# Eight SBUF places laid 448 bytes further, at another offset within a 512-byte line

## The chip, the cores and the metric

The kernel runs on one core of one Trainium2 chip. The metric is the device time of one execution in microseconds (us). TensorE (PE) does the matrix products; VectorE (DVE), ScalarE (ACT) and GpSimd (POOL) prepare operands and take results away; SyncE (SP) issues most DMAs. SBUF, the working memory, has 128 partitions; an array has the same byte address in each of them.

## The reference

One layer on 512 frames of width 1024, in float32:

```python
u = rms_norm(h, g_mix); z = u @ w_in            # q, k, v of two attentions, forget logits, two gates
y_a = sliding_window_attention(...) @ w_br_swa
y_b = forgetting_attention(...) @ w_br_fox
mixed = gates[0] * y_a + gates[1] * y_b
h = h + mixed @ w_mix_out                       # the merge's output projection
u = rms_norm(h, g_mlp)
h = h + jnp.square(jax.nn.relu(u @ w_ff1)) @ w_ff2
h = h + sigmoid(rms_norm(h, g_ple) @ w_ple_gate) * (p @ w_ple_proj)
return rms_norm(h, g_final)
```

## The kernel before

Every float32 product is done as three products of rounded parts: an operand is split into a high part (a rounded copy, made by ACT) and a low part (the rest, made by DVE), and PE computes high x high, high x low and low x high into the same PSUM tile (`mm3`, lines 72 to 75). A matmul has a stationary operand of 128 columns, which PE loads ahead of it, and a moving operand of up to 512 columns, which it streams. In the trace's names (out <- moving, stationary) the moving operand stands first.

The order of PE's and POOL's instructions is the order of the code; the other engines are scheduled by the framework, but for stretches in which their order is also the code's. The stages in order of time, with the names that PE's rows have:

- normalisation and the v projections, to 46 us (`va`, `vb`);
- both attentions (`h_sc`, `h_tr`, `h_pv`), filled up with the other projections (`pf`), to 214 us;
- branch projections (`psy`, moving `attn`) and half of the gates (`g`), to 298 us. The gates go through seven products instead of eight per 2x2 of blocks; the operands of products 3 and 7 (`u1_3`, `u1_7`) lie in four of the eight places named below, those of 5 and 6 elsewhere;
- the merge's output projection (`psm`), from 298 to 346 us: `mix` stationary, split weights of `w_mix_out` moving;
- embedding projection (`pspp`), to 359 us; its results lie in four of the eight places and go to HBM (`pp_spill`);
- the MLP, to 679 us: four rounds of ff1 (`f1`, split weights stationary, normed input moving, 256 columns) and ff2 (`s_..x`, `s_..y`, `s_..z`: the squared results `o2` of ff1 stationary, split weights of `w_ff2` moving, 512 columns); both in seven products. A step of ff1 has 24 matmuls, a step of ff2 has 12, and there are 56 steps of each;
- the embedding's gate (`psgt`, `psgl`), final norm and output.

The places that the change touches are eight buffers of 4096 bytes per partition in a pool of their own, each found by a tag `d0` to `d7`:

```python
    at2 = ctx.enter_context(tc.tile_pool(name="at2", bufs=1))
...
                mix[i] = at2.tile([P, 2, S], F32R, tag=f"d{i}", name=f"mix_{i}")
...
    OP_PLACE = {(0, 1): 0, (0, 5): 0, (0, 7): 0, (1, 1): 1, (1, 5): 1, (1, 7): 1, (0, 4): 2,
                (1, 4): 3, (0, 2): 4, (1, 2): 5, (1, 3): 5, (1, 6): 6, (0, 3): 7, (0, 6): None}
...
            t = at2.tile([P, 2, 2, 256], F32R, tag=f"d{n}", name=f"o2_{g}_{pn}")
```

`mix` and all of ff1's results lie there, but for the operand of product 6 in every other group of ff2 (`None` above: it lies in a buffer of another pool). The multiplication in ff2 is

```python
            for j in range(2):
                for n, (o, w) in enumerate(((oh, wh), (oh, wl), (ol, wh))):
                    nc.tensor.matmul(ps, o[:, j, ts_], w[:, j, :],
```

so `o` is stationary and `w` moving. The pools are laid one behind the other in SBUF, and within a pool a tag gets its place when it is first used. This gives every array an offset within a 512-byte line of its partition (its byte address modulo 512). Since slices are stepped by 512 bytes or multiples, an array keeps this offset in all its matmuls.

Of the kernel before, what the change touches and what calls it, by code (L numbers as in the profile page):

```python
# [8 lines left out]
F32 = mybir.dt.float32  # L9
# [5 lines left out]
P = 128  # L15
# [34 lines left out]
def layer_kernel(ctx: ExitStack, tc: tile.TileContext, x, p, g_mix, w_in, b_forget, swa_sinks,  # L50
# [794 lines left out]


    at2 = ctx.enter_context(tc.tile_pool(name="at2", bufs=1))
    look["wp2"] = ctx.enter_context(tc.tile_pool(name="wp2", bufs=2))
    look["split"] = 2
    n_mm = [0]  # L850
# [137 lines left out]
    for t in P2_STEPS:  # L988
# [8 lines left out]
        i = unit_of[t]  # L997
# [310 lines left out]
    for n, st_ in enumerate(steps):  # L1308
        res = None
        if done is not None:  # L1310
            if done[0] == "f1":
                res = win_out(done[:2], done[2], tmp)
                if res is not None:
                    src, dst, i, e = res
# [137 lines left out]
```

## Time and profile before

| what | value |
|---|---|
| median of three runs | 735.4 us (732.38, 735.40, 737.94) |
| the profiled execution, its own time | 736.25 us |
| its span in the trace | 734.2 us |
| outside the span | 2.05 us |
| granted clock, mean over the span | 0.998 of full speed |

The trace shows one execution, the one of 736.25 us. A matmul's row has a start and a duration; matmuls overlap, so the time that one costs is the distance from its start to the start of the next (called its spacing here), not its duration.

### The profile page before, as it was taken

Reading aid. Unit: us, or ns where it says so; the run is one execution under the profiler, and the core shown is the slowest. Engines: PE = TensorE matmul, PEld = TensorE weight load, DVE = VectorE, ACT = ScalarE, POOL = GpSimd, SP = SyncE. Lnnn points to the kernel's source line nnn. Section 1 sums busy time; section 2 is a strip of 40 time slices with the busy share of each in tenths; the row PEclk is TensorE's granted clock in tenths of the full one; section 3 lists DMA queues with packets and bytes.
Section 4 is the critical chain, followed back from the end, with each engine's and each line's share of the span. In section 5 each row is a group of like instructions: output and inputs, shape, how many; then the busy total and the mean of one; then the engine's idle time right before and its main releaser. Section 6 shows DMA issues by size and latency. Waiting matters only on the chain.

```text
span 734.2 us, 11456 instructions
## 1 busy us (share of the span) xinstructions
PE 721.4 (98%) x4234; PEld 635.9 (87%) x4234; DVE 530.7 (72%) x898; ACT 449.5 (61%) x838; POOL 86.2 (12%) x127
## 2 busy tenths in 40 slices
PE   9999999999999999999999999999999999999995
PEld 7998888888888998888889889988999889988884
DVE  4576888777697556546769985898669966997564
ACT  5457788879853553334777635774477546875452
POOL 1010211100001200002410102010300021010101
PEclk9999999999999999999999999999999999999999
DMA  8346455670364894530795598738894689069002
GB/s 254 93 131 160 113 145 145 151 194 1 116 217 99 172 344 145 200 115 19 234 211 197 107 276 171 224 88 248 185 252 111 153 225 226 33 144 341 4 25 90
DMA packets 73465, 116.72 MB, mean 159 GB/s; under 512 B 6593, under 2 KB 43969, under 8 KB 73410
## 3 DMA queue, kind: packets, MB, share of 16 engines
q1 hardware_dynamic: 65346, 86.64, 37.4%
q0 software_dynamic: 8064, 29.36, 21.0%
q8 instruction: 33, 0.54, 0.3%
q14 instruction: 22, 0.18, 0.1%
HBM read 72.93 MB, written 4.19 MB: 105 GB/s over the span
## 4 chain that ended last, share of the span: by engine, by line
PE 94%; DVE 2%; ACT 2%; DMA 1%; issue 1%; POOL 0%; POOLq 0%; DVEq 0%; ACTq 0%
PE pf L73 5%; PE pf L75 5%; PE pf L74 5%; PE s_6x L1269 3%; PE s_4x L1269 3%; PE s_2x L1269 3%; PE s_0x L1269 3%; PE h_sc L729 2%; PE h_pv L799 2%; PE h_tr L787 2%; PE psy L73 2%; PE psy L75 2%; PE psy L74 2%; PE psm L74 2%; PE psm L75 2%; PE psm L73 2%
## 5 line engine op out<-in xcount | busy, mean ns | idle before, releaser
L297 POOL DMA_DIRECT2D wq<-wq x26 | 23.5, 941 | 177.5 <-DVE u154l L324 27.1
L747 ACT ACTIVATE s<-s,h_nm 128x128 f32<-128x128 f32 (+1 forms) x64 | 32.6, 511 | 5.9 <-DVE h_nm L740 5.2
L358 POOL TENSOR_SCALAR n_ms<-acc 128x1 f32<-128x1 f32 x15 | 5.7, 381 | 171.3 <-ACT junk L1049 101.8
L70 DVE TENSOR_TENSOR h_ptl<-h_tr,h_pth 128x512 fp32r<-128x512 f32 (+2 forms) x40 | 22.9, 604 | 4.0 <-ACT h_pth L69 3.4
L69 ACT CAST u_h<-n_tr 128x512 fp32r<-128x512 f32 x22 | 12.2, 584 | 15.5 <-PE n_tr L378 7.6
L70 DVE TENSOR_TENSOR u_l<-n_tr,u_h 128x512 fp32r<-128x512 f32 x22 | 14.6, 686 | 8.2 <-ACT u_h L69 8.2
L69 ACT CAST h_pth<-h_tr 128x512 fp32r<-128x512 f32 (+2 forms) x40 | 19.4, 523 | 1.8 <-PE h_tr L787 1.4
L787 PE MATMUL h_tr<-ident,s 128*128 128x128 f32 x136 | 19.6, 277 | 0.2
L1049 ACT ACTIVATE junk<-h_sb 128x512 f32<-128x512 f32 x16 | 10.1, 629 | 15.6 <-DVE h_sb L1039 13.1
L297 POOL DMA_DIRECT2D wgw<-wgw x8 | 7.1, 970 | 101.7 <-DVE u25l L324 77.7
L1039 DVE TENSOR_TENSOR h_sb<-psm,h_sb 128x512 f32<-128x512 f32 x8 | 5.5, 690 | 16.4 <-PE psm L75 16.4
L799 PE MATMUL h_pv<-h_pth,v 128*128 128x256 f32 (+1 forms) x64 | 17.3, 291 | 0.0
L799 PE MATMUL h_pv<-h_ptl,v 128*128 128x256 f32 (+1 forms) x64 | 16.9, 305 | 0.4 <-DVE h_ptl L70 0.3
L787 PEld LDWEIGHTS h_tr<-ident,s 128*128 128x128 f32 x136 | 15.0, 141 | 2.0 <-DVE h_ao L809 0.5
L1358 DVE TENSOR_TENSOR sgp<-sgp,pp 128x512 f32<-128x512 f32 (+1 forms) x9 | 5.7, 633 | 15.2 <-ACT sgp L1357 15.2
L767 ACT ACTIVATE s<-s,h_rec 128x128 f32<-128x128 f32 (+2 forms) x32 | 14.2, 483 | 2.3 <-DVE h_rec L761 2.3
L809 DVE TENSOR_TENSOR h_ao<-h_pv,h_ao 64x512 f32<-64x512 f32 x16 | 10.9, 681 | 6.0 <-ACT h_ao L808 5.8
L735 DVE CUSTOM_DVE_ANT_0 s<-h_sc,causal 128x128 f32<-128x128 f32 (+3 forms) x32 | 13.8, 483 | 0.3 <-PE h_sc L729 0.3
L799 PEld LDWEIGHTS h_pv<-h_ptl,v 128*128 128x128 f32 x64 | 12.1, 188 | 1.7 <-DVE h_ptl L70 0.8
L1357 ACT ACTIVATE sgp<-psgt,rs 128x512 f32<-128x512 f32 x7 | 4.8, 685 | 14.2 <-PE psgt L75 14.2
L761 DVE RECIPROCAL h_rec<-h_den 128x4 f32<-128x4 f32 x16 | 3.0, 185 | 14.5 <-ACT s L747 14.3
L799 PEld LDWEIGHTS h_pv<-h_pth,v 128*128 128x128 f32 x64 | 12.1, 189 | 0.9
(1744 smaller groups left out, 2952.4 us busy)
## 6 DMA issues: line engine op xcount, KB each, us to landing
wq<-in_w_ff_dram SPq DMA_DIRECT2D x45, 512.0 KB, 5.5
wq<-wq POOLq DMA_DIRECT2D x26, 512.0 KB, 5.4
wq_c<-in_w_ff_dram SPq DMA_DIRECT2D x9, 512.0 KB, 6.2
wg<-in_w_in_dram SPq DMA_DIRECT2D x4, 1024.0 KB, 5.5
wgw<-in_w_in_dram SPq DMA_DIRECT2D x8, 512.0 KB, 4.9
wgw<-wgw POOLq DMA_DIRECT2D x8, 512.0 KB, 5.7
wmix<-in_w_mix_out_dram SPq DMA_DIRECT2D x4, 1024.0 KB, 5.3
wpg<-in_w_ple_gate_dram SPq DMA_DIRECT2D x4, 1024.0 KB, 9.4
```

The costliest lines, as they stand in the source:

```text
L69: nc.scalar.copy(hi, src)
L70: nc.vector.tensor_tensor(lo, src, hi.bitcast(F32), ALU.subtract)
L73: nc.tensor.matmul(ps, lh, rh, start=start, stop=False)
L74: nc.tensor.matmul(ps, lh, rl, start=False, stop=False)
L75: nc.tensor.matmul(ps, ll, rh, start=False, stop=stop)
L297: nc.gpsimd.dma_start(q, other, accum_op=ALU.add)
L729: nc.tensor.matmul(ps[:, off:off + n], qs[i][z][:, qb * P:(qb + 1) * P], kk[i][z][:, k0:k0 + n], start=z == 0, stop=z == 1)
L747: nc.scalar.activation(sl, sl, AF.Exp, bias=nm[:, qb:qb + 1], accum_out=den[:, qb:qb + 1])
L767: nc.scalar.activation(sl, sl, AF.Copy, scale=rec[:, qb:qb + 1])
L787: nc.tensor.transpose(tr[:, n, :], c["s"][:, o, :], ident)
L799: nc.tensor.matmul(pv[:, q0:q0 + nq, :], V2[kb][:, c["v"], :], t[:, o:o + nq, :], start=n == 0, stop=n == 2 * NT - 1, skip_group_check=True)
L1269: nc.tensor.matmul(ps, o[:, j, ts_], w[:, j, :], start=tg != "" and j == 0 and n == 0, stop=j == 1 and n == 2, skip_group_check=True)
```

## The change

Before the pool's first use, a tile of 448 bytes per partition is placed, then the eight places in the order of their tags, then a tile of 64 bytes. No instruction writes or reads the two small tiles or the `place_` names; they only take up room.

```diff
     at2 = ctx.enter_context(tc.tile_pool(name="at2", bufs=1))
+
+    at2.tile([P, 112], F32, name="line_a")
+    d_places = [at2.tile([P, 1024], F32, tag=f"d{i}", name=f"place_{i}") for i in range(8)]
+    at2.tile([P, 16], F32, name="line_b")
     look["wp2"] = ctx.enter_context(tc.tile_pool(name="wp2", bufs=2))
```

The program built from it has the same 7132 instructions, on every engine in the same order, with the same waits and the same semaphore values; only addresses differ. The pool began at byte 132352 of each partition (258 lines and 256 bytes); the places now begin at byte 132800 (259 lines and 192 bytes). Their order changes too: it was d2, d6, d3, d7, d0, d4, d1, d5, by first use, and is d0 to d7. All that lies behind the pool moves by 512 bytes and keeps its offset.

Offsets within a 512-byte line:

| array | part in the matmul | before | after |
|---|---|---|---|
| split weights (all `u..h`, `u..l` with a number) | stationary in `pf`, `psy`, `g`, `f1`; moving in `psm`, `s_`, `psgt` | 192 | 192 |
| normed inputs `u_h`, `u_l` | moving in `pf`, `g`, `f1`; stationary in `psgt` | 192 | 192 |
| `attn`, and what later lies in its places: operands of `f1` products 3, 5, 7; `wpp`, `pT` | moving in `psy`, `f1`; both in `pspp` | 256 | 256 |
| operands of `g` products 5 and 6 | moving | 256 | 256 |
| operands of `g` products 3 and 7 (in the eight places) | moving, 96 matmuls | 256 | 192 |
| `mix` (in the eight places) | stationary in `psm`, 192 matmuls | 256 | 192 |
| `o2` (in the eight places) | stationary in `s_`, 624 matmuls | 256 | 192 |
| `o2` of product 6, every other group | stationary in `s_`, 48 matmuls | 256 | 256 |
| `h_pth`, `h_ptl` and `v` in attention | moving and stationary in `h_pv` | 288 | 288 |

## Rows read from the trace of the kernel before

**Rows 1.** The page: busy time by engine, and the chain that ended last by engine.

```profile
PE 721.4 (98%) x4234; PEld 635.9 (87%) x4234; DVE 530.7 (72%) x898; ACT 449.5 (61%) x838; POOL 86.2 (12%) x127
...
PE 94%; DVE 2%; ACT 2%; DMA 1%; issue 1%; POOL 0%; POOLq 0%; DVEq 0%; ACTq 0%
```

**Rows 2.** Waits of PE, whole span: total us, times, longest us.

```profile
PE ('f1', 0)x L884 <- ACT u_('f1', 0)_4210 L895: 1.8, 1, 1.8
```

**Rows 3.** Stretches: length, then busy us by engine, clock, DMA share, GB/s.

```profile
298.00:346.00 48.00, 48.00 (x224) 39.09 (x223) 23.82 (x31) 18.55 (x33) 2.80 (x7) 1.00 0.36 121
...
441.00:476.00 35.00, 35.00 (x292) 34.77 (x291) 23.45 (x25) 24.37 (x33) 5.21 (x6) 1.00 0.82 203
476.00:520.00 44.00, 44.00 (x215) 36.60 (x214) 40.07 (x51) 24.61 (x33) 5.16 (x6) 1.00 0.68 175
```

**Rows 4.** PE in order of time, merge's output projection: start us, us.

```profile
322.01 0.39 PE L74 MATMUL psm<-u47l,mix 128*128 128x512 f32 x1
...
327.37 0.39 PE L73 MATMUL psm<-u47h,mix 128*128 128x512 f32 x1
```

**Rows 5.** The chain that ended last, ff2 stretch: start us, us, what.

```profile
483.49 2.80 PE s_2x L1269 x12
...
489.09 5.60 PE s_2z L1269 x24
```

**Rows 6.** PE in order of time, embedding gate: 24 spacings lie between these.

```profile
708.90 0.39 PE L73 MATMUL psgt<-u169h,u_h 128*128 128x512 f32 x1
...
714.34 0.39 PE L73 MATMUL psgt<-u169h,u_h 128*128 128x512 f32 x1
```

**Rows 7.** PE in order of time, embedding projection: 16 spacings lie between these.

```profile
348.17 0.39 PE L73 MATMUL pspp<-wpp0h,pT_h 128*128 128x512 f32 x1
...
351.79 0.39 PE L74 MATMUL pspp<-wpp0l,pT_h 128*128 128x512 f32 x1
```

**Rows 8.** PE in order of time, branch projections: 23 spacings in each pair.

```profile
225.22 0.39 PE L73 MATMUL psy<-attn,u23h 128*128 128x512 f32 x1
...
230.49 0.39 PE L75 MATMUL psy<-attn,u23l 128*128 128x512 f32 x1
...
281.70 0.40 PE L73 MATMUL psy<-attn,u40h 128*128 128x512 f32 x1
...
287.07 0.40 PE L75 MATMUL psy<-attn,u40l 128*128 128x512 f32 x1
```

**Rows 9.** PE in order of time, within attention, around transposes.

```profile
153.94 0.40 PE L799 MATMUL h_pv<-h_pth,v 128*128 128x512 f32 x1
...
154.40 0.34 PE L799 MATMUL h_pv<-h_pth,v 128*128 128x384 f32 x1
...
155.17 1.06 PE L787 MATMUL h_tr<-ident,s 128*128 128x128 f32 x8
...
156.30 0.40 PE L74 MATMUL pf<-u_l,u13h 128*128 128x512 f32 x1
...
158.16 0.39 PE L73 MATMUL pf<-u_h,u13h 128*128 128x512 f32 x1
```

**Rows 10.** The chain that ended last, ff1 stretch: start us, us, what.

```profile
454.98 2.88 PE ('f1', 3)y L884 x24
...
466.46 2.83 PE ('f1', 2)z L884 x24
```

**Rows 11.** The chain that ended last, gates: a step of product 2, one of 7.

```profile
250.66 2.88 PE ('g', 1, 2)y L884 x24
...
259.19 2.83 PE ('g', 0, 2)x L884 x24
```

**Rows 12.** The chain that ended last, first ff1 steps: start us, us, what.

```profile
369.35 7.31 DMA wq<-wq
...
383.65 0.49 ACT u_('f1', 0)_4210 L895
...
384.18 3.09 PE ('f1', 0)x L884 x24
```

## The prediction

> **What bounds the kernel now.** I read the page first: PE is busy 98% of the span, and 94% of the chain that ended last is PE's [rows 1]. So time is won only where PE's own instructions stand closer together, or where PE waits. Its waits come next: the longest is 1.8 us, once, in the first ff1 steps [rows 2]. The windows say the same by stage: in the merge's output projection, in ff1 and in ff2, PE is busy for the whole stretch at a granted clock of 1.00, which is the 2.4 GHz level, while DVE is the next, with 40.07 of 44.00 us in ff2 [rows 3].
>
> That leaves the spacing of matmuls, and there the reader should compare streams of one shape. All of the following have 128 rows, 128 columns and 512 moving columns. `psm` takes (327.37 - 322.01) / 23 = 233.0 ns each [rows 4]; ff2 takes 2.80 / 12 and 5.60 / 24, 233.3 ns [rows 5]. `psgt`, which runs through the same helper with the same kind of moving weights, takes 5.44 / 24 = 226.7 ns [rows 6], and `pspp` 3.62 / 16 = 226 ns [rows 7]. What differs is where the operands lie. In `psm` and ff2 the moving operand is at offset 192 and the stationary one at 256; in `psgt` both are at 192, in `pspp` both at 256. So it isn't that 256 is a bad place: equal offsets go with 226.7, unequal ones with 233.3. `psy` (256 against 192) blurs this: 5.37 / 23 = 233.5 ns late, but 5.27 / 23 = 229.1 ns early, with the same offsets [rows 8]. So the offset isn't all that decides.
>
> **The change part by part.** No instruction, order or wait changes; what is to be costed are three groups of matmuls whose offsets change, and the shift of everything else.
>
> *Stationary at 192 in `psm` and ff2.* 192 + 624 = 816 matmuls of 512 columns go from unequal (256 against 192) to equal (192, 192). At 233.3 - 226.7 = 6.6 ns each this is 816 x 6.6 = 5.4 us, all on PE's path: 1.3 us in `psm`, 4.1 us in ff2. The 48 matmuls of product 6 whose operand lies elsewhere stay as they are.
>
> *What an entrance costs.* Equal offsets don't give 226.7 at once. After attention's transposes a `pf` stream, equal at 192, runs 8 spacings in 1.86 us, 232.5 ns each [rows 9]. Against 226.7 that is 0.05 us for an entrance. `psm` has five (its start and four batches of transposes), 0.25 us; ff2 is entered twice a round from ff1 and once after the unequal step, 12 times, without transposes, 0 to 0.6 us. I take 0.2 us there, since ff1's own equal steps show no such start-up: 2.88 us for 24, right behind steps of another kind [rows 10]. Together 0.45 us given back.
>
> *Gate operands at 192.* 96 matmuls of 256 columns go from unequal to equal, and at 256 columns the trace has it the other way round: in ff1 the steps with equal offsets (`y`) take 2.88 / 24 = 120.0 ns, those with unequal ones (`z`, 256 against 192) 2.83 / 24 = 117.9 ns [rows 10]. The gates show both kinds themselves: 2.88 us for a step with equal offsets, 2.83 us for the step of product 7, whose operand now moves to an equal one [rows 11]. Four steps are 96 matmuls: cost 96 x 2.1 = 0.2 us.
>
> *What might take the gain back.* The 1.3 us of `psm` come ahead of the one place where PE waits: a weight block's sum by DMA, 7.31 us from issue to landing, then ACT, then PE at 384.18 [rows 12]. This DMA starts after work that itself follows PE's first ff1 steps, so it starts earlier too, and I cost it at nothing; if it were held by something that doesn't move, 1.3 us would be lost. In ff2, 14 steps a round shrink by up to 14 x 0.08 = 1.1 us of 44.00; DVE's 40.07 us [rows 3] still fit into the remaining 42.9, so the splits stay hidden behind PE. If that cover went, DVE would hold each round at its 40.07, which is further than this change reaches.
>
> *All else.* Writes of `mix`, of ff1's results and of the embedding projection's results go to new addresses on engines that PE doesn't wait for in these stretches [rows 2, 3]; the order of the places among themselves changes nothing that has a row. Nothing, between -0.1 and +0.1 us.
>
> Sum: -5.4 + 0.45 + 0.2 = -4.75, rounded to -4.7 us. The profiled execution took 736.25 us, so it would take 731.5. It is 0.85 us above the median of the three runs, 735.4; from the median the same sum gives **730.7 us**.
>
> **A rule that speaks against it.** By the rows above, equal and unequal offsets differ by 6.6 ns at one shape and one clock. The Trainium skill (SBUF — State Buffer, Who interferes with whom) gives PE two independent read ports, one for the moving operand and one for the weight load, and says that PE never waits on anyone; by that, how two operands lie to each other shouldn't matter and the change is worth 0. These rows disagree with it, unless something else than the offset separates the streams, which is the first rival.
>
> **The rivals.** *Nothing changes* (735.4 us): the streams differ for another reason, say that results of the squaring and weights of the gate are laid or timed differently, and the offset is only its companion. For it: early and late `psy`, 229.1 and 233.5 ns at the same offsets [rows 8]. Against it: `psm` and `psgt` share helper, shape and the array that moves, and two different equal offsets give the same spacing [rows 4, 6, 7]. It includes the case that the change doesn't do what it says, if the line that counts were longer than 512 bytes.
>
> *Slower* (737.0 us): an equal pair can also run in a slow pattern. `h_pv` is equal at 288 and takes 0.46 us for two spacings of 512 columns, 230 ns, within 5 ns of rounding, so up to 235 [rows 9]; the entrance of `pf` shows 232.5. If ff2, which alternates with 256-column steps, locked into 235 ns for good, 816 x 1.7 = 1.4 us would be lost, and 0.2 us in the gates: 735.4 + 1.6. It decides once the spacing is above 233.3 ns. Against it: every long undisturbed equal stream in the rows is at 226 to 227 [rows 6, 7].
>
> *Half the gain* (732.4 us): the new streams settle at the early `psy`'s 229.1 ns, 816 x 4.2 = 3.4 us, less 0.2 in the gates and 0.2 for entrances: 3.0 us. I count it with the forecast's range.
>
> *More* (728.8 us): no entrance costs anything, 5.2 us, and a shift in the first ff1 steps frees 1.4 of the 1.8 us that PE waits there [rows 2]: 6.6 us in all.
>
> **How the numbers follow.** Chances: forecast 0.52, half the gain 0.14, nothing 0.20, slower 0.07, more 0.07. The three runs lie between 732.38 and 737.94, so a median may be off by some 2 us. The range from 727.5 to 736.4 us reaches from below *more* by 1.3 us to past *nothing* by 1.0 us, and leaves out *slower* and the outer ends of the scatter. About 1% is what a measurement of this kernel can tell from no change; 1% of 735.4 is 7.35 us, under 728.05. The forecast's 4.7 us lies within that: 0.16 for faster by over 1% (scatter of the forecast, half of *more*), 0.81 within 1%, 0.03 slower by over 1%.
>
> **What would show it.** In the profile after, a `psm` group of 24 should take 5.44 us instead of 24 x 0.233 = 5.59, and a step of ff2 2.72 us instead of 2.80; one step of 12 a round should stay at 2.80. The gate steps of products 3 and 7 should go from 2.83 to 2.88 us. `psgt`, `pspp`, `psy` and ff1 should read as before. DVE's and ACT's rows should stand still. I'm wrong if ff2 stays at 2.80 us (the offset is a companion), if it goes to 2.82 (a slow pattern), or if ff2 shortens but the span doesn't, with new PE waits for ACT or DVE in ff2 or a longer one at 384 us.

## The result, and the profile after

The changed kernel took 731.22 us, the median of 22 runs (727.39 to 733.16); the kernel before, run beside it, 735.07 us (22 runs, 732.27 to 738.15). The ratio is 0.9946, with an interval of [0.9931, 0.9961]: 3.9 us less, where 4.7 were forecast. The interval, 2.9 to 5.1 us, lies clear of no change. The profiled execution of the changed kernel has a span of 730.1 us against 734.2, with a granted clock of 0.996. The page after, its line of busy times, answers to the first of [rows 1]:

```profile
PE 717.1 (98%) x4234; PEld 636.1 (87%) x4234; DVE 529.9 (73%) x898; ACT 449.3 (62%) x838; POOL 86.6 (12%) x127
```

PE is as full as before and has 4.3 us less to do; the other engines stand still. So the gain is PE's spacing, as it should be. The merge's output projection, PE in order of time, start and duration, answers to [rows 4]; 24 spacings lie between the two rows:

```profile
321.52 0.39 PE L73 MATMUL psm<-u47h,mix 128*128 128x512 f32 x1
...
326.96 0.39 PE L73 MATMUL psm<-u47h,mix 128*128 128x512 f32 x1
```

That is 5.44 / 24 = 226.7 ns, where there were 233.0. The chain that ended last, one round of ff2, answers to [rows 5]:

```profile
482.02 2.75 PE s_2x L1273 x12
484.77 2.72 PE s_2y L1273 x12
487.49 5.49 PE s_2z L1273 x24
492.99 2.72 PE s_2y L1273 x12
495.70 5.55 PE s_2x L1273 x24
501.25 2.72 PE s_2z L1273 x12
503.97 5.44 PE s_2x L1273 x24
```

A step takes 2.72 us where it took 2.80. The fifth row holds product 6, whose operand stayed at 256, and the step behind it: 2.80 + 2.75. The same chain in ff1, for [rows 10], reads as before, and in the gates, for [rows 11], the step of product 7 went from 2.83 to 2.88 us:

```profile
453.56 2.88 PE ('f1', 3)y L888 x24
...
465.03 2.83 PE ('f1', 2)z L888 x24
```

```profile
250.77 2.88 PE ('g', 1, 2)y L888 x24
...
259.30 2.88 PE ('g', 0, 2)x L888 x24
```

PE's longest wait, for [rows 2], and the chain through the first ff1 steps, for [rows 12]:

```profile
PE ('f1', 0)x L888 <- ACT u_('f1', 0)_4220 L899: 2.0, 1, 2.0
```

```profile
368.61 7.48 DMA wq<-wq
...
383.08 0.49 ACT u_('f1', 0)_4220 L899
383.61 3.09 PE ('f1', 0)x L888 x24
```

The stretch of [rows 3] that lies in ff2, with DVE's busy time third:

```profile
476.00:520.00 44.00, 44.00 (x228) 37.70 (x227) 40.30 (x51) 24.21 (x30) 5.17 (x6) 1.00 0.70 178
```

Laid out by the start of each stage, after minus before, the traces give this account. It is at +0.03 us when `pf` begins and at +0.11 when the gates do. The gates bring it to +0.33 when `psm` begins; `psm` to -0.76 (346.79 to 346.02 us); ff1's first round, with its longer wait, to -0.57 at ff2 (395.59 to 395.03); the four rounds of ff2 take 0.87, 0.88, 0.88 and 0.89 us off, and at the end it is -4.06.

### The profile page after: what moved, and what is told of

It is laid out like the page before. It is cut to its first block, busy times and chain, and to the rows that moved or that the text cites. A ratio compares the mean times of both kernels' runs of the same rounds, so it can differ in the third digit from the quotient of the medians.

```text
span 730.1 us, 11456 instructions
## 1 busy us (share of the span) xinstructions
PE 717.1 (98%) x4234; PEld 636.1 (87%) x4234; DVE 529.9 (73%) x898; ACT 449.3 (62%) x838; POOL 86.6 (12%) x127
## 4 chain that ended last, share of the span: by engine, by line
PE 93%; DVE 2%; DMA 2%; ACT 1%; issue 1%; POOL 0%; SPq 0%; POOLq 0%; DVEq 0%; ACTq 0%
PE pf L73 5%; PE pf L75 5%; PE pf L74 5%; PE s_6x L1273 3%; PE s_0x L1273 3%; PE s_4x L1273 3%; PE s_2x L1273 3%; PE h_sc L729 2%; PE h_pv L799 2%; PE h_tr L787 2%; PE psy L73 2%; PE psy L75 2%; PE psy L74 2%; PE psm L75 2%; PE psm L73 2%; PE psm L74 2%
## 5 line engine op out<-in xcount | busy, mean ns | idle before, releaser
L735 DVE CUSTOM_DVE_ANT_0 s<-h_sc,causal 128x128 f32<-128x128 f32 (+3 forms) x32 | 13.8, 482 | 0.3 <-PE h_sc L729 0.3
L761 DVE RECIPROCAL h_rec<-h_den 128x4 f32<-128x4 f32 x16 | 3.0, 185 | 14.5 <-ACT s L747 14.3
```

## The experiments

All of these kernels have the instructions, the order and the waits of the kernel before; only addresses differ. Their traces show the same instructions on each engine, with the same semaphore operations. The table has the offset within a 512-byte line of the operands, and the mean spacing in ns, start to next start, worked out from all undisturbed rows of a kind, those without a wait or another kind of instruction between them (some 450 spacings of `pf`, 183 of `psm`, some 610 of ff2, 96 of the gates, some 760 of ff1's equal steps before). "s, d" stands for the split weights and the eight places; the ff2 column leaves product 6 out. The ratio is the record's estimate over runs taken beside the kernel before, and not the quotient of the two medians, which can differ from it by 0.003 (e10_u2by32: 0.9924).

| kernel | s, d | `psm` | ff2 | gates 3 and 7 | ratio to before |
|---|---|---|---|---|---|
| before | 192, 256 | 233.3 | 233.4 | 117.7 | |
| after | 192, 192 | 227.4 | 227.6 | 120.0 | 0.9946 [0.9931, 0.9961] |
| e1_order | 192, 256 | 233.3 | 233.4 | 117.8 | 1.0011 [0.9988, 1.0034] |
| e2_off320 | 192, 320 | 232.8 | 232.4 | 118.2 to 119.4 | 0.9971 [0.9948, 0.9995] |
| e3_off448 | 192, 448 | 227.6 | 227.6 | 120.0 | 0.9930 [0.9908, 0.9952] |
| e4_off64 | 192, 64 | 233.1 | 232.4 | 118.3 to 119.1 | one run |
| e5_off224 | 192, 224 | 233.2 | 233.2 | 116.6 | one run |
| e7_w256 | 256, 256 | 227.2 | 227.1 | 120.0 | 0.9941 [0.9915, 0.9967] |
| e8_u2 | 256, 256 | 227.0 | 227.3 | 120.0 | 0.9903 [0.9878, 0.9927] |
| e9_all192 | 192, 192 | 227.2 | 227.3 | 120.0 | 0.9934 [0.9904, 0.9963] |
| e10_u2by32 | 224, 224 | 227.4 | 227.5 | 120.0 | 0.9898 [0.9862, 0.9935] |

**The order of the places alone (e1_order).** The change does two things: it reorders the places and shifts them. This keeps the first alone.

```diff
-    at2.tile([P, 112], F32, name="line_a")
     d_places = [at2.tile([P, 1024], F32, tag=f"d{i}", name=f"place_{i}") for i in range(8)]
-    at2.tile([P, 16], F32, name="line_b")
```

> The eight places are laid in the order of their tags, as after the change, but begin at byte 132352 as before (offset 256); the two small tiles are left out. Theory (equal or unequal offsets set the spacing): psm and ff2 stay at 233.3 ns a matmul, a step of ff2 at 2.80 us, time as before, ratio 1.000 within 0.2%. Rival (the places' order or neighbours made the gain): 226.7 ns, 2.72 us, ratio 0.995.

735.81 against 734.97 us, and every spacing as before. The order changes no spacing; what changes them is the shift.

**Which line, and does it need equality (e2_off320, e3_off448, e4_off64, e5_off224).** The first tile is sized 16, 48, 80 or 120 words instead of 112, and the second such that all behind the pool stays where the change has it. The places then stand at 320, 448, 64 and 224, that is +128, +256, -128 and +32 from the weights at 192.

```diff
-    at2.tile([P, 112], F32, name="line_a")
+    at2.tile([P, 48], F32, name="line_a")
     d_places = [at2.tile([P, 1024], F32, tag=f"d{i}", name=f"place_{i}") for i in range(8)]
-    at2.tile([P, 16], F32, name="line_b")
+    at2.tile([P, 80], F32, name="line_b")
```

> As after the change, but with 64 bytes in front and 448 behind: the places at offset 320, 128 bytes from the weights' 192. Theory with a line of 512 bytes: unequal, 233 ns in psm and ff2, a step of ff2 2.80 us, ratio 1.000. Rival (the line that counts is 128 bytes, or any distance but 64 is good): 226.7 ns, 2.72 us, ratio 0.995.

> As after the change, but with 192 bytes in front and 320 behind: the places at offset 448, 256 bytes from the weights' 192. Theory with a line of 512 bytes: unequal, 233 ns, 2.80 us a step of ff2, ratio 1.000. Rival (a line of 256 bytes): 226.7 ns, 2.72 us, ratio 0.995.

> As after the change with 320 bytes in front: the places at offset 64, 128 bytes below the weights' 192. With a line of 256 bytes this is the same as offset 320: psm and ff2 at 232.4 to 232.8 ns, gate products 3 and 7 at 118 to 119 ns. With a line of 512 bytes it would be another distance, with a spacing of its own.

> As after the change with 480 bytes in front: the places at offset 224, 32 bytes above the weights' 192. Theory (only equal offsets in a line of 256 bytes are good): 233 ns in psm and ff2. Rival (what counts is that both lie in the same 64 or 128 bytes): 226.7 ns.

At 256 bytes apart (e3_off448) the ff2 chain reads as after the change, at 128 apart (e2_off320) it has almost the old steps. The chain that ended last, same round, of e3_off448 and then of e2_off320:

```profile
481.67 2.72 PE s_2y L1273 x12
...
492.55 5.55 PE s_2x L1273 x24
498.09 2.72 PE s_2z L1273 x12
```

```profile
482.42 2.79 PE s_2y L1273 x12
...
493.57 5.59 PE s_2x L1273 x24
499.16 2.79 PE s_2z L1273 x12
```

So at the distances tried it is the distance modulo 256 that counts, not the offset in a 512-byte line. -128 gives nearly what +128 gives, and 32 bytes give nothing (ff2 at 233.2, one run): it takes equality, nearness doesn't help. The ratio of e3_off448 agrees with this. e2_off320's 0.9971 is more than its spacing gives: from `pf` on its trace is 1.7 us shorter than that of before, 0.55 by the spacing and 1.1 by a shorter wait in the first ff1 steps, 0.7 us in its profile against 1.8 [rows 2], which the spacing doesn't explain. Its interval, some 0.4 to 3.8 us, takes in either sum.

**The same from the other side (e7_w256).** If the distance decides, the places may stay at 256 and the weights move there. A 64-byte tile ahead of all weights does it, and it makes `pf`, `psgt` and the 256-column products that read the normed input unequal on the way: the normed inputs stay at 192, and what lies behind the weights moves by 64.

```diff
+    line = ctx.enter_context(tc.tile_pool(name="line", bufs=1))
+    line.tile([P, 16], F32, name="line_c")
...
+    at2.tile([P, 112], F32, name="line_a")
+    d_places = [at2.tile([P, 1024], F32, tag=f"d{i}", name=f"place_{i}") for i in range(8)]
```

> All that lies behind the normed inputs moves by 64 bytes, so the split weights lie at 256; the eight places and all behind them lie at 256 too, the normed inputs stay at 192. Now psm and ff2 are equal at 256 (all 864 matmuls), while pf and psgt (normed input against weights) become unequal, as do the ff1 and gate products of 256 columns that read the normed input. Theory (equality decides, not the place): psm and ff2 at 226.7 ns, ff2's steps 2.72 us, pf's and psgt's long streams at 233.3 instead of 226.7, ff1's x and y steps 2.83 instead of 2.88 us; against before -4.9 (psm, ff2) + 2.3 (pf) + 1.0 (psgt) - 1.6 (ff1) = -3.2 us, ratio 0.9956. Rival (192 is a good place for what is stationary): psm and ff2 stay at 233.3, pf and psgt change little, ratio 1.00 or above.

729.63 against 734.97 us. `psm` and ff2 are at 227, and product 6, whose operand now stands at 256 as well, at 226.7 (233.2 after the change). `pf`, made unequal (192 against 256), lost what ff2 won per matmul; PE in order of time, 24 spacings, in e7_w256 and then in the kernel before:

```profile
49.61 0.39 PE L75 MATMUL pf<-u_h,u0h 128*128 128x512 f32 x1
...
55.21 0.39 PE L75 MATMUL pf<-u_h,u1h 128*128 128x512 f32 x1
```

```profile
49.73 0.39 PE L74 MATMUL pf<-u_l,u0h 128*128 128x512 f32 x1
...
55.17 0.39 PE L74 MATMUL pf<-u_l,u1h 128*128 128x512 f32 x1
```

5.60 / 24 = 233.3 against 5.44 / 24 = 226.7 ns. This is the sharpest evidence: the shift that speeds one stream slows another, by the same 6.6 ns. `psgt` is the miss: unequal too (256 against 192), it went only to 229.0. In `psgt` the moving operand stands 64 bytes above the stationary one, in `pf` 64 below; so either the direction counts, or what ran before it decides. No run here tells these apart for `psgt`. In ff2 a new thing shows, in the waits of the weight loads:

```profile
PEld s_2z L1274 <- DVE o L72: 0.6, 1, 0.6
```

With all steps shorter, DVE's split is now just late at the fifth step.

**Product 6 too (e9_all192).** The change without its second small tile: the buffers behind the pool move by 64, and the operands of the gates' products 5 and 6 and of ff2's product 6 come to 192.

```diff
-    at2.tile([P, 16], F32, name="line_b")
```

> As after the change without the 64 bytes behind the places, so that the pools behind them lie at 192 too: ff2's product 6 in every other group is equal, and gate products 5 and 6. Theory: the step of product 6 takes 2.72 instead of 2.80 us, and the step behind it 2.72 instead of 2.75, -0.4 us over four rounds; gates 96 x 2.1 = +0.2 us; ratio 0.9943. If entrances into ff2 cost nothing beyond what an unequal step leaves, the first steps behind ff1 fall to 2.72 as well; the theory has them stay at 2.75.

730.23 against 735.29 us. Product 6 and the step behind it take 2.72 us each, the gates' steps of 5 and 6 go to 120.0 ns. The steps at ff2's entrances stay at 2.76 and 2.75: what an entrance costs is not product 6's doing. It depends on the step ahead of it: in e7_w256 and e8_u2, where ff1's `x` and `y` steps are unequal, the second entrance costs nothing (2.72 us).

**Both gains at once (e8_u2, e10_u2by32).** ff1's steps of equal offsets are 256 columns wide, and there the unequal ones are the faster [rows 10]. So the weights, the places and attention's inputs are made equal at 256, and the MLP's input alone is left at 192. Beside the first tile and the places as in e7_w256, without the tile ahead of the weights, the two halves of the normed input become one tile with 16 spare words, which also move all behind it by 64 bytes.

```diff
-        return (up.tile([P, KT, S], F32R, tag="u_hi", bufs=1, name=name + "_h"),
-                up.tile([P, KT, S], F32R, tag="u_lo", bufs=1, name=name + "_l"))
+        both = up.tile([P, 2 * KT * S + 16], F32R, tag="u_both", bufs=1, name=name)
+        o = 0 if name == "u2" else 16
+        return [both[:, o + i * KT * S:o + (i + 1) * KT * S].rearrange("q (k s) -> q k s", s=S)
+                for i in range(2)]
```

> Built on the changed kernel: the normed input and the weights go to 256, but the MLP's normed input lies 64 bytes lower, at 192; places and all behind them at 256. So all matmuls of 512 columns but psy's are equal, and ff1's 768 matmuls that read the MLP's normed input become unequal at 256 columns. Theory (256 columns: unequal is 2.1 ns cheaper): ff1's x and y steps 2.83 instead of 2.88 us, -1.6 us; the 48 matmuls of product 6 equal, -0.3 us, one entrance a round less, -0.1; gate products 5 and 6 equal, +0.2; in all -1.8 us against the change, -5.9 us and ratio 0.992 against before. Rival (DVE and ACT, or the weight sums by DMA, set the MLP's pace by now): ff1 shortens, PE's waits in ff2 and at the first ff1 steps grow by as much, ratio 0.9945.

728.06 against 735.29 us, ratio 0.9903: ahead of the changed kernel's 0.9946 as well (the intervals don't overlap, though the two didn't run side by side), and with the next one the fastest layout tried. From `pf` on its trace is 6.6 us shorter than that of before, where the changed kernel's is 4.1. The chain of e8_u2, one ff1 step and ff2's round:

```profile
477.86 2.83 PE ('f1', 3)x L889 x24
480.68 2.72 PE s_2x L1274 x12
483.40 2.72 PE s_2y L1274 x12
486.12 5.54 PE s_2z L1274 x24
491.66 2.72 PE s_2y L1274 x12
494.38 5.44 PE s_2x L1274 x24
```

The ff1 step is at 2.83 us (2.88 before), product 6 at 2.72; of the ff2 steps shown, only the fifth, 2.82 of the row with 5.54, is over. e10_u2by32 is the same with 8 words in place of the two 16s, so that the MLP's input stands 32 bytes from the weights and not 64.

> As e8_u2 (moving and stationary operands of psm, ff2 and both later merges equal at one offset within 256 bytes, the MLP's 256-column f1 x and y matmuls unequal), but all of it 32 bytes lower: weights, split places and the merge's input at 224, the MLP's input at 192, so that f1 x and y stand 32 bytes apart instead of 64. Theory (spacing goes by the distance modulo 256): the 512-column groups stay at 226.7 to 227.5 ns; f1 x and y at 32 apart go from 117.8 to 116.6 ns, the figure that e5_off224 showed for the 256-column products 3 and 7 at 32 apart; 16 groups of 48 f1 x and y matmuls x 1.2 ns = 0.9 us less than e8, ratio to before about 0.989. Rival 1 (it is only equal or unequal that counts for 256 columns, and 116.6 belonged to something else of e5): f1 x and y stay at 117.8, ratio 0.990 as in e8. Rival 2: the faster f1 steps only lengthen the waits for the normed, activated operand at ff1's entrance and for the split behind ff2's fourth step; ratio 0.990 with f1 x and y at 116.6.

728.71 against 734.29 us, ratio 0.9898, with an interval that doesn't tell it from e8_u2; from `pf` on its trace is 5.8 us shorter than that of before, against 6.6. ff1's `x` and `y` steps ran at 118.3 ns, not at 116.6: the expectation carried over a figure of e5_off224's gates, where the moving operand stands above the stationary one and not below, and the size of the distance alone doesn't foretell a 256-column spacing. What holds for 256 columns in all these runs is less: the equal steps take 120 ns, and the unequal ones less.

## Why the prediction was right, step by step

**Direction and mechanism: right, and now shown.** Offset and time were only seen together in the rows of before. The runs separate them: the order without the shift does nothing, distances of 128 and 32 do next to nothing, another place at the same distance modulo 256 does everything, and moving the weights to the places does it too, while `pf` loses what they win. The rival *nothing changes* is out, and *slower* as well: the long equal streams settled at 226.7, at 192, at 224, at 256 and at 192 against 448. The time alone would not have decided: the range took in *nothing* and *half the gain*, and 3.9 us lies between the forecast's 4.7 and half the gain's 3.0. It is the 226.7 ns that speak for the forecast and against half the gain's 229.1. What in PE or in the memory makes it so, no run here shows. By the Trainium skill (SBUF — State Buffer, SBUF: two separate sides), under which PE never waits on anyone, the change would be worth 0, if that is taken to hold between the two operands of one matmul too; ff2's step of 2.72 us instead of 2.80 speaks against that reading.

**`psm`: right.** -1.27 + 0.25 for entrances was forecast, -1.09 came.

**ff2: the mis-sized term.** A round holds 13 steps that become equal, 13 x 12 x 6.6 ns = 1.03 us; it took off 0.88. So 0.15 us a round was given back, 0.6 in all, and not the 0.2 that I took from bounds of 0 to 0.6. The argument for the low end, that ff1's own equal steps show no start-up [rows 10], was the weak one: those are 256-column steps, and the nearer row was the 512-column `pf` after transposes at 232.5 ns [rows 9]. The rows show where it goes: the two steps that stand straight behind ff1's take 2.76 and 2.75 us, the one behind product 6 2.75, and the fifth 2.77. The first three are the entrances, 0.10 us a round, 0.4 in all: twice what I took. The fifth, another 0.05 us in most rounds, is no entrance: the low part of its operand comes from DVE at the last moment. All engines in order of time, after the change:

```profile
489.58 0.68 DVE L70 TENSOR_TENSOR o<-z_('f1', 3)_4912,o 128x512 fp32r<-128x512 f32 x1
...
490.32 0.38 PEld L1273 LDWEIGHTS s_2z<-u99h,o 128*128 128x128 f32 x2
```

DVE ends at 490.26, and the weight load that needs the result stands at 490.32, 0.27 us behind the load before it; the 0.6 us wait in e7_w256 shows the same openly. So the prediction's "the splits stay hidden", which costed this at nothing, was too simple. DVE's sum fits, 40.30 of 44.00 us after the change, but one split of it falls due early.

**The gates: right.** 0.2 us was forecast, 0.21 came, by 2.83 to 2.88 us a step.

**The first ff1 wait: costed at nothing, and +0.17.** Its DMA did start earlier (368.61 for 369.35 us) but took 7.48 for 7.31 us, and the wait grew from 1.8 to 2.0 us. It wasn't held in place, so the gain of `psm` was not lost. But this wait came out between 0.7 and 2.3 us over all the profiles, so 0.17 us is within what it does by itself.

**The sum.** -1.09 + 0.17 - 3.52 + 0.21, and under 0.2 us over all other stages, is the span's -4.06. The terms were -5.4 + 0.45 + 0.2; the difference is what ff2 gave back beyond the forecast (0.4, of it some 0.2 by entrances and 0.2 by the late split) and that wait (0.17).

**A premise that was wrong.** The prediction spoke of the line of 512 bytes. For the offsets of the change that makes no difference, so the forecast didn't suffer, but by a line of 512 bytes e3_off448 would be unequal and stay at 233 ns; it ran at 227.6.

## What to carry to other kernels

When PE is full and its matmuls of one shape run at two spacings, list for each stream the byte address of the moving and of the stationary operand modulo 256: for 512 columns with a weight load each, equal ones ran 6.6 ns (2.9%) closer here, for a few unused bytes and no instruction. Do the list for all streams, since a shift moves whatever lies behind it: the same 64 bytes helped ff2 and slowed `pf`, and 256-column streams ran closer when unequal (117.8 against 120.0 ns). Price each change of stream, not only the steady stretch, and look for the operand that becomes late first when the steps shrink.

## What the runs showed that I had not expected

**Unequal streams have more than one spacing at the same addresses; what chooses it stays open.** Late `psy` ran at 233.4 ns in seven profiles and at 228.9 in e7_w256, e8_u2, e9_all192 and e10_u2by32, in e9_all192 with its own offsets untouched (256 against 192). In ff1 it can be seen to switch. The chain of e7_w256, unequal steps ahead of and behind a short hold of PE (in the row of 2.97):

```profile
459.61 2.83 PE ('f1', 3)x L889 x24
462.44 2.97 PE ('f1', 2)x L889 x24
465.41 2.72 PE ('f1', 2)z L889 x24
468.13 2.72 PE ('f1', 3)x L889 x24
470.85 2.72 PE ('f1', 3)z L889 x24
```

After the hold the steps take 2.72 us, 113.3 ns a matmul instead of 117.8, and e9_all192 does the same behind its own. Yet the wait of 2.0 us at 383 us after the change is followed by steps of 2.83. Nor is a hold needed: in e7_w256's gates, where PE waits for nothing, an unequal step of product 2 takes 2.74 us behind equal steps of 2.88. e3_off448 switches to 2.72 too, behind a stretch in which its granted clock fell to 0.50, the level of 1.2 GHz. That was from 380.6 to 384.0 us; from 377 to 379 us PE had been busy for 0.49 us only; it is the only profile with such a fall within the layer, and it lost 1.2 us there. The early and late `psy` of [rows 8], which the prediction couldn't place, are of this kind. In e8_u2 to e10_u2by32 all gate steps ahead of late `psy` are equal, and in e7_w256 the last one runs at 113.3 ns; in the seven others some of them are unequal and the last runs at 120.0. So what ran before seems to choose, but by what rule isn't shown. This second spacing also gave e7_w256 to e10_u2by32 part of a gain that the distances don't: about 0.4 us of late `psy`.

**The start has two lengths.** In four of the eleven profiles the first 12 us are 3.2 us shorter. The same four matmuls, in the kernel before and in e3_off448, PE in order of time:

```profile
5.02 3.78 PE L490 MATMUL g_ps<-g_row,ones_row 1*128 1x512 f32 x4
```

```profile
5.02 2.01 PE L490 MATMUL g_ps<-g_row,ones_row 1*128 1x512 f32 x4
```

The views print a granted clock of 1.00 for both, but that is no reading: the trace's clock records begin only at 13.8 us in the kernel before and at 5.1 us in e3_off448, each at 1.00, the level of 2.4 GHz. In the four short profiles they begin at 5.0 to 5.1 us, in the other seven at 13.0 to 14.3 us. Ahead of that record the 128-column warm-up matmuls stand 213 ns apart, behind it 109 ns, as they do from 6.96 us on in e3_off448 and not yet at 8.73 us in the kernel before. So the start is long where TensorE comes to the upper level late, though PE is busy from 1.4 us on in both. What sets the moment stays open. Nothing ties it to the layout: e2_off320, e3_off448, e4_off64 and e9_all192 have it, e5_off224 and the changed kernel, which lie between them in layout, don't, and the runs of the kernel before scatter by about as much (732.27 to 738.15 us). The kernel before and the changed one both have the long start, so the -4.06 us between their spans is free of it. Otherwise single spans of these kernels can be compared only from `pf` on, and the ratios rest on many runs.
